# Final norm written whole, the last slot's tokens normed by themselves and written behind it; slot 31 run wholly behind slot 30

## The chip, the cores and the metric

One NeuronCore of a Trainium2 chip runs the whole kernel. The metric is the device time of one execution in microseconds; the time before is the median of three runs. "PE" is TensorE, "DVE" VectorE, "ACT" ScalarE, "POOL" GpSimd and "SP" SyncE; PEld is TensorE's weight load. A "q" behind an engine's name is its sequencer, which issues DMAs and waits on semaphores.

## What is computed

Two transformer blocks on 1024 tokens of width 1024, in float32. The change touches the end of the second one: the routed experts' sum is added to the residual, and every token is normed.

```python
def hierarchical_moe(h, ...):          # 32 experts, two per token
    ...
    out = lax.map(run_block, ...)       # (silu(x @ w_gate) * (x @ w_up)) @ w_down
    out = out * slot_gate[:, None]
    y = jnp.zeros((n_tok, dm)).at[slot_tok].add(out, mode='drop')
...
        x = x + gate_f * hierarchical_moe(h, ...)
    return rms_norm_2(x, final_g)       # x * rsqrt(mean(x*x) + 1e-6) * final_g
```

## The kernel before

**Slots.** The second block's 32 experts are run one behind the other as slots, ordered by how many tokens chose them. The last six slots (26 to 31) hold at most 64 tokens each ("small", `HALF_AT`), two others at most 32. For a slot the kernel gathers its tokens' rows (POOL, `xg`), turns them (PE, line 541; ACT, line 543), multiplies them with the gate and up weights (line 556), applies Silu (line 671) and the product (line 672), turns the hidden rows, multiplies with the down weights, copies half of the result from PSUM (line 563), scales by the token's gate (lines 687, 688) and adds the rows into the residual `acc_d` in DRAM with an indirect accumulating DMA from POOL (line 518). Each such scatter waits until the one before it has landed.

**Weights.** Each weight matrix of a slot is loaded in two chunks of 1 MB; a small slot uses two gate, two up and two down chunks in fp32 as they are. `Loader` issues them on SP's queue in the order in which the units will run (`unit_order`, `queue_experts`), at most four in flight: load n waits until load n-4 has landed. Buffers come from four rings: two first ones (`rawA`, `rawS`, two buffers each) and two of five buffers behind them. `keep_first_rings(2)` keeps the last two chunks out of the first rings.

**Order of units.** `unit_order` puts slot i's down product behind slot i+1's gate and up products. So at the end it runs: gate/up of 30, down of 29, gate/up of 31, down of 30, down of 31. The order of every engine's instructions is the order in which the program emits them.

**The last slot.** When slot 30's scatter has been issued, `load_sums` (line 1409) takes the four buffers of the first rings as `xs`, eight residual tiles of 128 tokens, and issues their loads on SP (line 1407); these wait for slot 30's scatter to land. It also loads `final_g` on ACT's queue (line 1418) and builds `at`, a one-hot matrix from the last slot's tokens to their rows (lines 1424 to 1426). Slot 31's result isn't scattered: `keep_rows` (line 1430) splits it into a high and a low part, `rows`.

**The If.** Line 1449 is a branch on `nx`, the number of extra blocks needed when an expert has more tokens than its slots hold. Here it isn't taken. Every engine loads `nx` and branches, and behind it engines wait for some of their outstanding DMAs.

**The final norm.** Behind the If: for each tile, `add(tt)` adds `at` x `rows` to the residual tile. Even tiles are added on DVE from PSUM (line 1473), odd ones on PE with an identity matmul (lines 1466, 1468). ACT squares and sums (line 1476), Ln and Exp give the factor (lines 204, 205), DVE multiplies (line 1486), SP stores (line 1487). `add` runs two tiles ahead. `use_ln_exp` (line 155) loads ACT's function table ahead of it.

Of the kernel before, what the change touches and what calls it, by code (L numbers as in the profile page):

```python
# [21 lines left out]
P = 128  # L22
# [100 lines left out]
def kernel(ctx, tc, a, out):  # L123
# [38 lines left out]
    def bcast_row(ap, n):  # L162
        return bass.AP(tensor=ap.tensor, offset=ap.offset, ap=[[0, P], [1, n]])
# [421 lines left out]
    def run_experts(hlp, blocks, route):  # L585
# [1 line left out]

        n = len(blocks)
        units = []
        for i, kind in unit_order(n):  # L590
            units += [(i, kind, c) for c in blocks[i][kind]] if kind in "gud" else [(i, kind, None)]
        todo = deque((u[2][0], part) for u in units if u[2] is not None and not blocks[u[0]].get("small") for part in range(N_PARTS))
        hls, raws = deque(), {}
# [47 lines left out]
        def few(i, kind, c):  # L641

            nonlocal ps, gate_raw
            s = blocks[i]["subs"][0]
            m = s["m"]
            key, _, ci, n_ch, _ = c
            raw = ld.take(key)
            if key[2] == "g":
                gate_raw = key, raw
                if ci == 0:  # L650
                    ps = mm_ps()[:, 0]
                return
            if kind == "u":
                for b in range(4):
                    ex.product_few(s["xT"], (raw[:, b], gate_raw[1][:, b]), ps, ci * 4 + b, 7)
                ld.done(gate_raw[0])
            else:
                if ci == 0:
                    ps = mm_ps()[:, 0]
                for b in range(2):  # L660
                    ex.product_few(s["hT"], [raw[:, b, h * 512:(h + 1) * 512] for h in range(2)], ps, ci * 2 + b, 3)
            ld.done(key)
            for _ in range(N_PARTS):
                if len(hls) < N_SPLIT:
                    ahead()
            if ci < n_ch - 1:
                return
            if kind == "u":
                s["hid"] = hid = ex.tile("hid", [fd], ex.wide)[:m]
                if m == P // 2:  # L670
                    nc.scalar.activation(hid, ps[m:], AF.Silu)
                    nc.vector.tensor_tensor(hid, ps[:m], hid, op=OP.mult)
                else:
                    up = ex.few_sums(ps, m, (None, hid))
                    nc.scalar.activation(hid, hid, AF.Silu)
                    nc.vector.tensor_tensor(hid, up, hid, op=OP.mult)
                return
            if "keep" in s:
                upper = ex.tile("whole", [512], 1)[:m]
                ex.few_sums(ps, m, (None, upper))  # L680
                s["keep"](ps[:m], s, 0)
                s["keep"](upper, s, 1)
                return
            y = ex.tile("yo", [D], ex.wide)
            if m == P // 2:
                ex.few_sums(ps, m, (None, y[:m, 512:]))
                nc.vector.scalar_tensor_tensor(y[:m, :512], ps[:m], s["gate"][:m], ex.grow[:m, :512], op0=OP.mult, op1=OP.mult)
                nc.vector.scalar_tensor_tensor(y[:m, 512:], y[:m, 512:], s["gate"][:m], ex.grow[:m, 512:], op0=OP.mult, op1=OP.mult)
            else:
                ex.few_sums(ps, m, (y[:m, :512], y[:m, 512:]))  # L690
                nc.vector.scalar_tensor_tensor(y[:m], y[:m], s["gate"][:m], ex.grow[:m], op0=OP.mult, op1=OP.mult)
            ex.scatter(y, s["idx"], m)
            if "after" in s:
                s["after"]()
# [48 lines left out]
                    if "after" in s:  # L743
                        s["after"]()

    def unit_order(n):
        for i in range(n + 1):
            if i < n:
                yield from ((i, "g"), (i, "u"), (i + 1, "xT"))
            if i > 0:  # L750
                yield i - 1, "d"
            if i < n:
                yield i, "hT"
# [14 lines left out]
    dyn_ids, slot_row = {}, {}  # L768

    def queue_experts(blocks):  # L770
        for i, kind in unit_order(len(blocks)):
            for key, w, c, _, n in blocks[i][kind] if kind in "gud" else ():
                ld.queue(key, [P, 2048 // n, n], chunk_src(w, c, n))

# [371 lines left out]
    def block2(x_src):  # L1146
# [209 lines left out]
                b["u"] = [c for both in zip(b["g"], b["u"]) for c in both]  # L1356
                b["g"] = []
        queue_experts(blocks)
        keep_first_rings(2)
        s4 = ctx.enter_context(ExitStack())  # L1360

        def after_wo0():
# [8 lines left out]
        with ExitStack() as s3:  # L1371
# [37 lines left out]
            def load_sums():  # L1409
                ex, sub = lists[0][1], blocks[-1]["subs"][0]  # L1410
                m = sub["m"]
                assert not ld.todo and all(p[3] == 0 for p in ld.pools[:2])
                for pool in (rawA, rawS):
                    for _ in range(2):
                        xs.append(pool.tile([P, 2048], F32, tag="raw", name="raw").rearrange("p (t d) -> p t d", t=2))
                load_xs(nc.sync)
                fin["g"] = ex.tile("xg", [D], ex.n_x)
                nc.scalar.dma_start(fin["g"], bcast_row(a["final_g_2"], D))

                both = ex.tile("xT", [2, D], ex.wide, F32R)  # L1420
                rows, at = both[:2 * m, 0], both[:2 * m, 1]
                d = ex.tile("whole", [ex.fdim], 1)[:2 * m, :NT + 1]
                for i in range(2):
                    nc.vector.tensor_copy(d[i * m:(i + 1) * m, NT:], sub["idx"][:m])
                nc.vector.tensor_scalar(d[:, :NT], C["io"][:2 * m, 0:NT], -float(P), d[:, NT:], op0=OP.mult, op1=OP.add)
                nc.vector.tensor_tensor(at.rearrange("p (t c) -> p t c", t=NT), C["io"][:2 * m, None, :].to_broadcast([2 * m, NT, P]),
                                        d[:, :NT, None].to_broadcast([2 * m, NT, P]), op=OP.is_equal)
                fin["rows"], fin["at"], fin["y"] = rows, at, ex.tile("yo", [D], ex.wide)

            def keep_rows(ps, s, h):  # L1430
                m, rows = s["m"], fin["rows"]
                c = slice(h * 512, (h + 1) * 512)
                y = fin["y"][:m, c]
                nc.vector.scalar_tensor_tensor(y, ps[:m], s["gate"][:m], lists[0][1].grow[:m, c], op0=OP.mult, op1=OP.mult)
                nc.scalar.copy(rows[:m, c], y)
                nc.vector.tensor_tensor(rows[m:, c], y, rows[:m, c].bitcast(F32), op=OP.subtract)

            run_experts(hlp, blocks, route2)
            r, ex = lists[0]
            ld.drop_pools()  # L1440
            s4.close()

            nx = nc.values_load(r["nx"][0:1, 0:1], min_val=0, max_val=N_EXTRA)
            with ExitStack() as s5:
                ep = sub_pool(s5, "ep2")
                hlp = sub_pool(s5, "xhl3", bufs=3)
                ex3 = Experts(ep, ep, h_d[1], acc_d[1], None, 512, 1)
                ex3.grow = ex.grow
                with tc.If(nx > 0):
                    further = extra_lists(ep, r)  # L1450
                    with tc.For_i(0, nx, 1) as i:
                        extra_block(ex3, ep, hlp, i, further, *ws)
                    load_xs(nc.gpsimd)

            fp = sub_pool(s3, "fin")
            ss = fp.tile([P, NT], F32, name="ss")
            use_ln_exp()

            def add(tt):

                ps = mm_ps()
                x, s = xs[tt // 2][:, tt % 2], ss[:, tt:tt + 1]
                on_pe = tt % 2 == 1
                if on_pe:
                    for h in range(2):
                        nc.tensor.matmul(ps[:, h], ident, x[:, h * 512:(h + 1) * 512], start=True, stop=False)
                for h in range(2):
                    nc.tensor.matmul(ps[:, h], fin["at"][:, tt * P:(tt + 1) * P], fin["rows"][:, h * 512:(h + 1) * 512],
                                     start=not on_pe, stop=True)
                if on_pe:  # L1470
                    sums[tt] = flat(ps)
                else:
                    nc.vector.tensor_tensor(x, x, flat(ps), op=OP.add)
                    sums[tt] = x
                junk = fp.tile([P, D], F32, tag="junk", name="junk", bufs=2)
                nc.scalar.activation(junk, sums[tt], AF.Square, accum_out=s)
                rstd_of(s)

            sums = {}
            add(0)  # L1480
            add(1)
            for tt in range(NT):
                if tt + 2 < NT:
                    add(tt + 2)
                x, s = xs[tt // 2][:, tt % 2], ss[:, tt:tt + 1]
                nc.vector.scalar_tensor_tensor(x, sums[tt], s, fin["g"], op0=OP.mult, op1=OP.mult)
                nc.sync.dma_start(tok_tile(out[0], tt), x)

    gates_out = []

# [530 lines left out]
```

## Time and profile before

| | us |
|---|---|
| median of 3 runs | 2077.5 (2076.21 to 2079.62) |
| the profiled execution | 2075.67 |
| its span, first to last instruction | 2073.7 |
| slot 30's scatter issued | 2041.04 |
| residual loads issued from | 2046.51 |
| first / last product of the final norm starts | 2057.26 / 2067.88 |
| first / last output store issued | 2060.26 / 2069.19 |

All times of a trace count from the span's start. Over the whole span PE is busy 91%, PEld 72%, DVE 72%, ACT 50%, POOL 18%. A wait is put down by the profile to the last event that preceded its end, which need not be its cause.

### The profile page before, as it was taken

How to read it: one execution, taken by the hardware profiler on the slowest of the kernel's cores; microseconds unless marked ns; L12 is line 12 of the kernel's file. 1: busy time of each engine (PE TensorE's matmuls, PEld its weight loads, DVE VectorE, ACT ScalarE, POOL GpSimd, SP SyncE). 2: the span in 40 equal slices, each digit the busy share in tenths (PEclk: the TensorE clock that was granted, in tenths of full speed). 3: DMA queues.
4: the chain of work that ended last, by engine and by line, in shares of the span. 5: the costliest groups of instructions: out<-in, count | busy, mean ns of one | idle time of the engine just before them, and what ended most of it. 6: DMA issues, size and time to landing. Idle time of an engine off the chain costs nothing.

```text
span 2073.7 us, 25402 instructions
## 1 busy us (share of the span) xinstructions
PE 1895.3 (91%) x9192; PEld 1487.6 (72%) x9192; DVE 1500.4 (72%) x1934; ACT 1036.7 (50%) x1454; POOL 369.9 (18%) x300
## 2 busy tenths in 40 slices
PE   4999999949999999999969999899599999999885
PEld 3788888837888888888757787788488676776332
DVE  6699985466999999999844256676797768586214
ACT  4411123216788787878755244332386656465213
POOL 1045430032010101000010000000511314142210
PEclk7999999969999999999989999999799999999998
DMA  9467746288999999999532001335798999999997
GB/s 325 144 231 259 259 163 225 102 308 287 377 387 401 389 402 384 405 379 387 157 110 82 11 16 36 120 145 194 300 366 286 391 362 389 379 390 390 365 388 297
DMA packets 154108, 569.57 MB, mean 275 GB/s; under 512 B 31287, under 2 KB 54551, under 8 KB 104828
## 3 DMA queue, kind: packets, MB, share of 16 engines
q1 hardware_dynamic: 134812, 511.78, 64.3%
q0 software_dynamic: 18784, 55.46, 9.4%
q8 instruction: 73, 1.20, 0.2%
q10 hardware_dynamic: 384, 0.68, 0.1%
q14 instruction: 55, 0.45, 0.1%
HBM read 534.12 MB, written 42.66 MB: 278 GB/s over the span
## 4 chain that ended last, share of the span: by engine, by line
PE 76%; DMA 10%; DVE 9%; ACT 2%; issue 2%; POOL 0%; SPq 0%; DVEq 0%; ACTq 0%
PE mm L199 21%; PE mm L201 20%; PE mm L200 20%; DMA raw<-in_w_expert_up_dram 5%; DMA raw<-in_w_expert_down_dram 3%; DVE hl L192 2%; PE aux L533 2%; PE half L201 1%; PE half L200 1%; PE half L199 1%; PE aux L417 1%; PE mm L556 1%; PE aux L1599 1%; DVE adacc L301 1%; DMA raw<-in_w_expert_gate_dram 1%
## 5 line engine op out<-in xcount | busy, mean ns | idle before, releaser
L192 DVE TENSOR_TENSOR hl<-raw,hl 128x1024 fp32r<-128x1024 f32 x601 | 716.6, 1232 | 129.1 <-ACT hl L191 110.8
L191 ACT CAST hl<-raw 128x1024 fp32r<-128x1024 f32 x612 | 634.9, 1054 | 262.4 <-PE mm L201 228.2
L199 PE MATMUL mm<-hl,xT 128*128 128x512 f32 x832 | 327.8, 394 | 0.2 <-issue 0.2
L201 PE MATMUL mm<-hl,xT 128*128 128x512 f32 x832 | 325.2, 391 | 0.0
L200 PE MATMUL mm<-hl,xT 128*128 128x512 f32 x832 | 325.1, 391 | 0.0
L199 PE MATMUL mm<-hT,hl 128*128 128x512 f32 x448 | 178.7, 399 | 8.5 <-ACT hT L879 6.2
L201 PEld LDWEIGHTS mm<-hl,xT 128*128 128x128 f32 x832 | 156.6, 188 | 33.4 <-issue 0.4
L199 PEld LDWEIGHTS mm<-hl,xT 128*128 128x128 f32 x832 | 157.0, 189 | 32.5 <-issue 0.4
L200 PEld LDWEIGHTS mm<-hl,xT 128*128 128x128 f32 x832 | 156.7, 188 | 32.6 <-DVE hl L192 0.9
L200 PE MATMUL mm<-hT,hl 128*128 128x512 f32 x448 | 176.3, 393 | 0.5 <-DVE hT L880 0.5
L201 PE MATMUL mm<-hT,hl 128*128 128x512 f32 x448 | 176.0, 393 | 0.0
L199 PE MATMUL mm<-hl,hT 128*128 128x512 f32 x416 | 164.9, 396 | 0.2 <-ACT hT L195 0.2
L201 PE MATMUL mm<-hl,hT 128*128 128x512 f32 x416 | 162.6, 391 | 1.0 <-DVE hT L196 1.0
L200 PE MATMUL mm<-hl,hT 128*128 128x512 f32 x416 | 162.2, 390 | 0.0
L518 POOL DMA_INDIRECT acc_d<-yo,idx x35 | 64.3, 1836 | 259.1 <-DVE yo L741 118.2
L556 PE MATMUL mm<-raw,xT 128*32 128x512 f32 (+1 forms) x512 | 88.1, 630 | 21.6 <-DMA raw<-in_w_expert_up_dram 21.6
L199 PEld LDWEIGHTS mm<-hT,hl 128*128 128x128 f32 x448 | 85.1, 190 | 27.3 <-ACT hT L879 7.1
L301 DVE SCALAR_TENSOR_TENSOR adacc<-adaw,ccol,adacc 128x512 f32<-128x512 f32 x142 | 100.0, 770 | 0.0
L200 PEld LDWEIGHTS mm<-hT,hl 128*128 128x128 f32 x448 | 85.1, 190 | 18.9 <-DVE hT L880 1.5
L201 PEld LDWEIGHTS mm<-hT,hl 128*128 128x128 f32 x448 | 84.8, 189 | 17.9
L512 POOL DMA_INDIRECT xg<-h_d,idx x34 | 61.4, 1806 | 167.8 <-PE aux L541 112.6
L201 PEld LDWEIGHTS mm<-hl,hT 128*128 128x128 f32 x416 | 78.1, 188 | 17.9 <-DVE hT L196 1.4
(487 smaller groups left out, 3013.8 us busy)
## 6 DMA issues: line engine op xcount, KB each, us to landing
raw<-in_moe_w_gate_dram SPq DMA_DIRECT2D x64, 1024.0 KB
raw<-in_moe_w_up_dram SPq DMA_DIRECT2D x64, 1024.0 KB
raw<-in_moe_w_down_dram SPq DMA_DIRECT2D x64, 1024.0 KB
raw<-in_w_expert_gate_dram SPq DMA_DIRECT2D x64, 1024.0 KB
raw<-in_w_expert_down_dram SPq DMA_DIRECT2D x63, 1024.0 KB
raw<-in_w_expert_up_dram SPq DMA_DIRECT2D x62, 1024.0 KB
adaw<-in_ada_w_dram SPq DMA_DIRECT2D x47, 1024.0 KB
raw<-in_sc_w_in_dram SPq DMA_DIRECT2D x9, 1024.0 KB
```

What stands on the lines that cost most here:

```text
L191: nc.scalar.copy(hl[:, 0], raw)
L192: lo.tensor_tensor(hl[:, 1], raw, hl[:, 0].bitcast(F32), op=OP.subtract)
L199: nc.tensor.matmul(o, s_hi, m_hi, start=start, stop=False)
L200: nc.tensor.matmul(o, s_hi, m_lo, start=False, stop=False)
L201: nc.tensor.matmul(o, s_lo, m_hi, start=False, stop=stop)
L301: nc.vector.scalar_tensor_tensor(acc[kk % 2], w[:, k], c, add, op0=OP.mult, op1=OP.add)
L417: nc.tensor.matmul(o, xT[:, k], rsc[:, k], start=k == 0, stop=k == KC - 1)
L512: nc.gpsimd.indirect_dma_start(out=x[:m], out_offset=None, in_=self.src, in_offset=bass.IndirectOffsetOnAxis(ap=idx[:m], axis=0), bounds_c ...
L518: nc.gpsimd.indirect_dma_start(out=self.acc, out_offset=bass.IndirectOffsetOnAxis(ap=idx[:m], axis=0), in_=y[:m], in_offset=None, compute_ ...
L533: nc.tensor.transpose(ps[:, i * P:(i + 1) * P], self.block(x, k, tag), ident)
L556: nc.tensor.matmul(ps[at:at + m], sT[:, k], w, start=k < split, stop=k > last - split)
L1599: nc.tensor.matmul(ps[:, h * P:(h + 1) * P], a_, b_, start=True, stop=True)
```

## The change

Slot 30 is finished before slot 31 begins: `unit_order` gives its down product ahead of slot 31's gate and up products, and the six last chunks (four gate/up, two down of slot 31) are kept out of the first rings, since the residual is loaded into those as soon as slot 30 has been scattered. At that point POOL also gathers the residual rows of slot 31's tokens into `fin["x"]`.

The final norm then runs on the residual tiles without slot 31's contribution, in pairs of tiles (`normed`), ahead of the If, and all eight tiles are stored. Behind pair 1, slot 31's result is added to the gathered rows and these are normed too. When all eight stores have landed, POOL writes the normed rows over their places in the output with an indirect DMA. Should extra blocks be needed, the If's body scatters slot 31's result, runs them, and does the whole norm again.

```diff
-        for i, kind in unit_order(n):
+        for i, kind in unit_order(n, blocks[-1].get("small")):
...
             if "keep" in s:
                 upper = ex.tile("whole", [512], 1)[:m]
                 ex.few_sums(ps, m, (None, upper))
-                s["keep"](ps[:m], s, 0)
-                s["keep"](upper, s, 1)
+                s["keep"]((ps[:m], upper), s)
                 return
...
-    def unit_order(n):
+    def unit_order(n, alone=False):
+
         for i in range(n + 1):
+            if alone and i == n - 1:
+                yield i - 1, "d"
             if i < n:
                 yield from ((i, "g"), (i, "u"), (i + 1, "xT"))
-            if i > 0:
+            if i > 0 and not (alone and i == n - 1):
                 yield i - 1, "d"
...
-        for i, kind in unit_order(len(blocks)):
+        for i, kind in unit_order(len(blocks), blocks[-1].get("small")):
...
-        keep_first_rings(2)
+        keep_first_rings(6)
...
                 nc.scalar.dma_start(fin["g"], bcast_row(a["final_g_2"], D))
-
-                both = ex.tile("xT", [2, D], ex.wide, F32R)
...
+                fin["x"] = ex.tile("xg", [D], ex.n_x)[:m]
+                nc.gpsimd.indirect_dma_start(out=fin["x"], out_offset=None, in_=acc_d[1],
+                                             in_offset=bass.IndirectOffsetOnAxis(ap=sub["idx"][:m], axis=0),
+                                             bounds_check=T - 1, oob_is_err=False)
+
+            def keep_rows(parts, s):
+                m = s["m"]
+                fin["y"] = y = lists[0][1].tile("yo", [D], 2)[:m]
+                for h, p in enumerate(parts):
+                    c = slice(h * 512, (h + 1) * 512)
+                    nc.vector.scalar_tensor_tensor(y[:, c], p, s["gate"][:m], lists[0][1].grow[:m, c], op0=OP.mult, op1=OP.mult)
...
+            def normed(x, out_x, n):
+
+                p = x.shape[0]
+                ss = fp.tile([P, 2], F32, tag="ss", name="ss", bufs=4)[:p, :n]
+                for i in range(n):
+                    junk = fp.tile([P, D], F32, tag="junk", name="junk", bufs=2)[:p]
+                    nc.scalar.activation(junk, x[:, i], AF.Square, accum_out=ss[:, i:i + 1])
+                nc.scalar.activation(ss, ss, AF.Ln, bias=epsc[:p], scale=1.0 / D)
+                nc.scalar.activation(ss, ss, AF.Exp, scale=-0.5)
+                for i in range(n):
+                    nc.vector.scalar_tensor_tensor(x[:, i], x[:, i], ss[:, i:i + 1], fin["g"][:p], op0=OP.mult, op1=OP.mult)
+                    if out_x is not None:
+                        stores.append(nc.sync.dma_start(tok_tile(out[0], out_x + i), x[:, i]).ins)
...
+            stores = []
+            use_ln_exp()
+            for q in range(NT // 2):
+                normed(xs[q], 2 * q, 2)
+                if q == 1:
+                    nc.vector.tensor_tensor(fin["x"], fin["x"], fin["y"], op=OP.add)
+                    normed(fin["x"][:, None, :], None, 1)
+            rows = nc.gpsimd.indirect_dma_start(out=out[0], out_offset=bass.IndirectOffsetOnAxis(ap=last["idx"][:m], axis=0),
+                                                in_=fin["x"], in_offset=None, bounds_check=T - 1, oob_is_err=False).ins
+            behind(rows, stores)
+            stores.clear()
 
             nx = nc.values_load(r["nx"][0:1, 0:1], min_val=0, max_val=N_EXTRA)
...
                 with tc.If(nx > 0):
+                    ex.scatter(fin["y"], last["idx"], m)
                     further = extra_lists(ep, r)
...
                     load_xs(nc.gpsimd)
-
-            fp = sub_pool(s3, "fin")
...
+                    use_ln_exp()
+                    for q in range(NT // 2):
+                        normed(xs[q], 2 * q, 2)
+                    for st in stores:
+                        behind(st, [rows])
```

## Rows read from the trace of the kernel before

**Rows 1.** Busy time by stretch: PE, PEld, DVE, ACT, POOL, clock, DMA share, GB/s.

```profile
2010.00:2037.50 27.50, 21.58 (x104) 7.94 (x102) 2.77 (x4) 2.73 (x5) 2.59 (x2) 1.00 0.99 390
2037.50:2041.60 4.10, 3.58 (x19) 1.20 (x16) 2.16 (x6) 0.95 (x2) 0.56 (x1) 1.00 0.47 169
...
2048.00:2058.50 10.50, 8.24 (x18) 3.92 (x18) 4.03 (x5) 5.55 (x11) 0.00 (x0) 0.67 0.98 391
...
2061.00:2072.10 11.10, 4.15 (x12) 1.81 (x10) 8.16 (x7) 6.19 (x16) 0.00 (x0) 0.84 0.96 379
```

**Rows 2.** Scatters of slots 29 and 30: timeline, POOL's wait, chain of waits.

```profile
2025.01 1.40 POOL L518 DMA_INDIRECT acc_d<-yo,idx  x1 [13.82 <-DVE yo L688]
...
L518 POOLq EVENT_SEMAPHORE  x13: 17/17/17, 1872.5 to 2032.9; - x13
...
2041.04 5.46 DMA acc_d<-yo,idx
```

**Rows 3.** Timeline where the final norm starts: start, us, engine, line, operation, idle.

```profile
2050.34 1.22 DVE L1473 TENSOR_TENSOR raw<-raw,mm 128x1024 f32<-128x1024 f32 x1 [1.91 <-DMA raw<-acc_d]
...
2054.30 1.78 PE L1468 MATMUL mm<-xT 128*128 128x512 f32 x4
...
2056.12 1.22 DVE L1473 TENSOR_TENSOR raw<-raw,mm 128x1024 f32<-128x1024 f32 x1 [4.56 <-DMA raw<-acc_d]
```

**Rows 4.** Timeline: PE's waits for the second down chunks of slots 30 and 31.

```profile
2036.58 0.37 PEld L556 LDWEIGHTS mm<-raw,hT 128*64 128x64 f32 x4 [0.49 <-DMA raw<-in_w_expert_down_dram]
...
2041.58 0.20 PEld L556 LDWEIGHTS mm<-raw,hT 128*64 128x64 f32 x4 [0.69 <-DMA raw<-in_w_expert_down_dram]
```

**Rows 5.** Timeline: the load of `final_g` issued.

```profile
2038.81 0.36 ACTq L1418 DMA_DIRECT2D xg<-in_final_g_dram  x1
```

**Rows 6.** Timeline: a unit after a pause, then slot 31 from its last up chunk.

```profile
1975.17 5.35 PE L556 MATMUL mm<-raw,xT 128*64 128x512 f32 x16 [2.16 <-DMA raw<-in_w_expert_up_dram]
...
2031.61 3.65 PE L556 MATMUL mm<-raw,xT 128*64 128x512 f32 x16 [2.44 <-DMA raw<-in_w_expert_up_dram]
...
2035.31 0.59 ACT L671 ACTIVATE hid<-mm 64x512 f32<-64x512 f32 x1 [11.27 <-PE mm L556]
...
2035.94 0.68 DVE L672 TENSOR_TENSOR hid<-mm,hid 64x512 f32<-64x512 f32 x1 [11.21 <-ACT hid L671]
...
2038.63 0.69 PE L541 MATMUL aux<-ident,hid 64*128 64x64 f32 x4
...
2039.83 3.68 PE L556 MATMUL mm<-raw,hT 128*64 128x512 f32 x16 [0.52 <-ACT hT L543]
...
2043.56 0.58 ACT L563 COPY whole<-mm 64x512 f32<-64x512 f32 x1 [3.78 <-PE mm L556]
```

**Rows 7.** Timeline of ACT: a table load and what follows it.

```profile
1128.56 1.28 ACT L1242 ACT_TABLE_LOAD   x1
1129.85 2.01 ACT L1242 ACTIVATE y<-y 128x1024 f32<-128x1024 f32 x2
```

**Rows 8.** Timeline: one tile's factor on ACT; the last two products on DVE.

```profile
2057.38 1.06 ACT L1476 ACTIVATE junk<-raw 128x1024 f32<-128x1024 f32 x1
...
2058.56 0.29 ACT L204 ACTIVATE ss<-ss,epsc 128x1 f32<-128x1 f32 x1
...
2059.00 1.00 ACT L1476 ACTIVATE junk<-mm 128x1024 f32<-128x1024 f32 x1
...
2066.69 1.28 DVE L1486 SCALAR_TENSOR_TENSOR raw<-raw,ss,xg 128x1024 f32<-128x1024 f32 x1
2067.88 1.28 DVE L1486 SCALAR_TENSOR_TENSOR raw<-mm,ss,xg 128x1024 f32<-128x1024 f32 x1
```

**Rows 9.** The stores on SP's timeline; SP's drains at the program's end (ns, starts).

```profile
2060.26 9.26 SPq L1487 DMA_DIRECT2D out_dram<-raw  x8
...
L2017 SPq DRAIN  x3: 7/7/13, 2072.8 to 2073.1; - x3
```

**Rows 10.** POOL's semaphore update behind the If (ns; start).

```profile
L1449 POOLq INC_SWDGE_SEM  x1: 1626/1626/1626, 2046.8 to 2046.8; - x1
```

More of the change, by code (lines that the diff above doesn't have):

```diff
@@ L1418, in load_sums @@
                 nc.scalar.dma_start(fin["g"], bcast_row(a["final_g_2"], D))
-                both = ex.tile("xT", [2, D], ex.wide, F32R)
[L1421 to L1436, printed above, removed]
+                fin["x"] = ex.tile("xg", [D], ex.n_x)[:m]
[8 more added lines that the diff above has]
+                    nc.vector.scalar_tensor_tensor(y[:, c], p, s["gate"][:m], lists[0][1].grow[:m, c], op0=OP.mult, op1=OP.mult)
             run_experts(hlp, blocks, route2)
@@ L1441, in block2, with behind @@
             s4.close()
+            fp = sub_pool(s3, "fin")
+            last = blocks[-1]["subs"][0]
+            m = last["m"]
+            def normed(x, out_x, n):
[10 more added lines that the diff above has]
+                        stores.append(nc.sync.dma_start(tok_tile(out[0], out_x + i), x[:, i]).ins)
+            def behind(ins, earlier):
+                for e in earlier:
+                    tc.add_manual_dep(ins, e.name, DependencyInfo(DependencyClass.Sync, DependencyReason.DATA), reason="the same rows")
+            stores = []
[9 more added lines that the diff above has]
+            stores.clear()
             nx = nc.values_load(r["nx"][0:1, 0:1], min_val=0, max_val=N_EXTRA)
@@ L1453, in block2 @@
                     load_xs(nc.gpsimd)
-            fp = sub_pool(s3, "fin")
[L1456 to L1487, printed above, removed]
+                    use_ln_exp()
[3 more added lines that the diff above has]
+                        behind(st, [rows])
     gates_out = []
```

## Prediction

> **What bounds the kernel now.** I read the page first (span, engines), then the stretch table, then the timeline of the last 60 us, and last the waits of SP and POOL there. The page says PE 91% busy; that is an average over stages which the change leaves alone. What counts is the tail. [rows 1]: until 2037.5 us the DMA engines are full (0.99), so the slots' matmuls only follow the weights. Then their share falls (0.47 to 2041.6); they are full again with the residual's 4 MB from 2048 to 2058.5, and with the 4 MB of output from 2061 to 2072.1, and 1.6 us later the span ends. The reader should see two holes: 10.5 us ahead of the residual load and 2.5 us ahead of the stores. The first is made by slot 30's scatter [rows 2]: it is issued at 2041.04 and has landed 5.46 us later, at 2046.5, and only then does SP issue the residual's loads. The second is VectorE: `add(2)` on it stands ahead of the norm of tile 0 and starts at 2056.12 [rows 3]. That wait is put down to a DMA, but tile 1's and 2's matmuls run at the lower clock until 2056.1 (0.67 of full on average in 2048 to 2058.5), and the DVE add follows their end; from there VectorE is back to back until 2069.16.
>
> **The change, part by part.** Everything before slot 30's down product is untouched. I write u31b for the last gate/up chunk of slot 31, x for the residual tiles, fx for the last slot's own rows.
>
> *Weight order.* Now slot 31's four gate/up chunks come ahead of slot 30's two down chunks; afterwards behind them. Bytes and pace are the same (390 GB/s), so a chunk takes the landing time of whichever stood in its place. u31b moves from 2031.6 [rows 6] into the place where 30's second down chunk landed: 2036.6 [rows 4]. The last weight still lands near 2041.6. Keeping six chunks out of the first rings leaves them 10 buffers with 4 loads in flight; no load waits for a buffer. Price 0, and if that cover went, one chunk time, 2.6 us.
>
> *`final_g`.* Its 0.5 MB load is issued behind slot 30's copy on ScalarE, now at 2038.81, in the hole [rows 5]. It moves to about 2028.5, into the full stretch: 0.5 MB at 390 GB/s is 1.3 us which everything behind it is later. Bounds 0 and 1.3; I take 1.3 because that stretch has no free share. So u31b lands at 2037.9.
>
> *Slot 30 and the residual load.* Slot 30's second down chunk takes the second of the four places, two chunk times (1 MB at 390 GB/s is 2.7 us) before 2031.6, so 2026.3; half a unit of matmuls, the copy and two products later, about 4 us, its `yo` is done near 2030. POOL may not issue that scatter before slot 29's has landed, 2032.9 [rows 2]. It then takes 5.46 us (idle DMA) to 7.9 us (slot 29's, under load: 2025.01 to 2032.9): landed by 2038.5 to 2041. SP has by then issued all weights (the last one waits for the chunk four places before it, about 2033), so x starts at 2041 instead of 2046.5 and 4 MB take 10.4 us as now. The gather of fx waits for the same landing on POOL, where nothing is queued that anybody needs; it has until 2058.
>
> *Who gets the 5.5 us?* Nobody, at first: on ScalarE the norm stands behind all of slot 31, and that is later. Slot 31 loses its cover (slot 30's down product, which now hides its transposes). By [rows 6]: u31b to `Silu` 3.70, to hid 1.31, transposes and copy to the first down matmul 1.2, 16 matmuls 3.73, copy 0.58, small gaps 0.1: 10.6 us, 2048.5. Now the same copy ends at 2044.1. Then the table load, 1.28 us, which today lies beside the wait for x: ScalarE starts on x at 2049.8. By then pair 0 has landed (2041 + 1.5 + 2.6, even with the 4 us that the slowest DMA engine lags: 2049.1).
>
> An earlier table load starts at 1128.56 and takes 1.28 us, and the next activation starts at 1129.85 [rows 7]: nothing stands between them. The Trainium skill, "ScalarE: Activation LUTs", What ACT_TABLE_LOAD costs, gives a load of about the same size plus a drain of 1.38 us with each switch of set; by it the end would be 1.4 us later. The rows show none behind the load, and they decide.
>
> *The norm.* Removed: all matmuls of lines 1466 and 1468, four adds, the one-hot and the split rows; so the PE clock no longer matters there. The new order costs ScalarE per pair two squares of 1.18 us with their read, and Ln and Exp, 0.44 to the next start: 2.80 us, against 3.24 for two tiles now [rows 8]. VectorE needs two times 1.19, so ScalarE sets the pace. Pairs 0 and 1: 2049.8 to 2055.4. Then fx stands in both queues: its add waits on VectorE for both products of pair 1 (2.5 us with the handover) and takes 1.22 itself [rows 3], and ScalarE's square of fx waits for the add: idle from 2055.4 to 2059.2, then 1.62 of its own, 2060.9. Pairs 2 and 3 end at 2066.5, the last product at 2069.1. That is the time at which it ends now (2069.16).
>
> *The tail that is added.* The last store goes out at 2069.2 as now; its packets end at 2072.1 and the final drains run from 2072.8 [rows 9], so POOL, which waits for all eight stores, starts at about 2072.2. Queued behind that wait are POOL's load of `nx`, the branch, and the end of the program, for which all engines wait. The plain indirect write isn't in the trace. Bounds: 5.46 us for the accumulating one on a quiet DMA, 3.8 us from the first x load's issue at 2046.5 to its first use at 2050.34 [rows 3]; I take 4.6: 2076.8. Now the If stands in the hole ahead of the norm; behind its branch POOL waits for its DMAs and spends 1.63 us on a semaphore update, from 2046.8, 0.3 us behind the scatter's landing [rows 10]. At the end nothing covers this: 0.3 + 1.63, bounds 0 and 1.9, I take 1.9, the row of the same block: 2078.7. End barrier 0.9 as now: 2079.6.
>
> The Trainium skill, "DMA: Bandwidth & Descriptors", Anatomy of one DMA, fits such a transfer by 2.0 us plus bytes over 436 GB/s; an estimate for 64 rows of 4 KB by that page is 2.6 us, which would end the kernel 2 us earlier. The one quiet indirect write of this trace took 5.46, so I stay with the rows.
>
> **Sum.** 2037.9 + 10.6 + 1.3 (start on x) + 16.7 (four pairs, fx and its stall) + 2.6 (last product) + 3.1 (last store) + 4.6 + 1.9 + 0.9 = 2079.6 against 2073.7: 5.9 us longer. The profiled execution took 2075.67, so 2081.6 beside it; the median of the runs shown is 2077.5, so I forecast 2083.4.
>
> **Rivals.**
> 1. *The weight stream loses its lag; not slower.* Bytes run at full rate until 2037.5 but the last chunk is usable only at 2041.58 and the share is 0.47 in between [rows 1, 4]: one slow DMA engine is 4 us behind. If the new order lets it catch up, u31b lands 4 us earlier and all of the sum moves with it: 2079.4. It decides from a lag under 2.2 us on. Against it: slot 29's scatter and its small packets stay where they are, slot 30's comes on top.
> 2. *The tail is cheap.* The plain write lands in 3.8, and the If's update is run while it flies: 1.9 + 0.8 less, 2080.7. For it: nothing of POOL needs that order; against it: today's waits on POOL come ahead of the update.
> 3. *A cold PE.* With pauses of over 2 us ahead of it, a 16 matmul unit takes 5.35 instead of 3.65 at 1975 [rows 6]. After 2027.7 such pauses surround u31a, u31b and the down product. One or two units at half clock cost 1.7 to 3.4: 2085.1 to 2086.8.
> 4. *The overlap comes true.* If ScalarE could start on x as it lands, near 2045, and pair 2 stood ahead of fx, 3 to 5 us would go. Program order on ScalarE speaks against it: all of slot 31 is issued first. Even rivals 1 and 2 with a free `final_g` give together 2075.4, within 0.2% of now; being faster needs a term that I don't see.
>
> **How the numbers follow.** 0.2% is 4.2 us here, about what a measurement of this kernel can tell from no change, so slower begins at 2081.7. Forecast 0.58 (a sixth of it, with short tail terms, falls under 2081.7), rival 1 0.13, rival 2 0.11, rival 3 0.10, rival 4 or a gain unseen 0.08. Slower 0.48 + 0.10 = 0.58, same 0.10 + 0.13 + 0.11 = 0.34, faster 0.08. The range goes from 2077.0 (rival 1 with most of rival 2) to 2089.0 (rival 3 in full with the slow end of the scatter and the spread).
>
> **What the profile would show.** Slot 31's Silu at about 2041.6 (with u31b landed at 2037.9), x loads issued at 2041, the table load at 2048.5, ScalarE idle for 3.8 us ahead of the square of fx, the last product at 2069, POOL's indirect write at 2072, and after it 1.6 us of POOL's update. The forecast is wrong if u31b lands by 2034, if ScalarE squares x before slot 31's last copy, or if the span ends within 3 us of the write's issue.

## The result, and the profile after

The changed kernel takes 2092.93 us in the median (2087.42 to 2094.58) beside 2076.21 us of the kernel before: ratio 1.0072, 95% interval 1.0059 to 1.0085. Run again beside other variants it took 2090.25 us against 2076.16: ratio 1.0070 (1.0057 to 1.0083). It is about 15 us slower; 2083.4 was forecast, with a range to 2089.0.

The span of its profiled execution is 2091.1 us, 17.4 longer than before. First the lead: how late this execution already was ahead of everything altered. The load of slot 30's second up chunk is the same instruction in both. The kernel before, SP's timeline:

```profile
2004.42 0.33 SPq L92 DMA_DIRECT2D raw<-in_w_expert_up_dram  x1
```

The same load in the changed kernel:

```profile
2010.07 0.33 SPq L92 DMA_DIRECT2D raw<-in_w_expert_up_dram  x1
```

So 5.65 us of the 17.4 lie ahead of it, and 11.7 behind. From here on "lead" is that load's distance to 2004.42, and "behind" is a span less 2073.7 less its lead. The load is a good mark: less the lead, the products on slot 31's last up chunk start between 2037.8 and 2037.9 in all seven profiled executions with the new order. The experiments below show what the lead is.

The stretch behind, in the changed kernel; columns as in [rows 1]:

```profile
2010.00:2043.50 33.50, 25.05 (x120) 9.35 (x120) 5.57 (x8) 4.83 (x9) 4.23 (x3) 1.00 1.01 400
2043.50:2049.50 6.00, 4.34 (x20) 1.61 (x20) 0.68 (x1) 0.74 (x2) 0.99 (x1) 1.00 0.45 104
2049.50:2060.20 10.70, 3.65 (x16) 1.06 (x16) 3.44 (x4) 6.85 (x13) 0.00 (x0) 0.79 1.01 365
2060.20:2066.50 6.30, 0.00 (x0) 0.00 (x0) 4.36 (x5) 2.50 (x8) 0.00 (x0) 0.50 0.95 389
2066.50:2070.80 4.30, 0.00 (x0) 0.00 (x0) 2.94 (x3) 4.24 (x10) 0.00 (x0) 0.50 0.01 6
2070.80:2077.00 6.20, 0.00 (x0) 0.00 (x0) 2.99 (x3) 0.57 (x3) 0.00 (x0) 0.50 0.87 342
2077.00:2091.10 14.10, 0.00 (x0) 0.00 (x0) 0.00 (x0) 0.00 (x0) 0.95 (x1) 0.50 0.07 14
```

The last line is the one to look at: 14.1 us in which POOL works for 0.95, no other engine at all, and the DMA moves next to nothing. In [rows 1] and [rows 9] the span ended 1.6 us behind the last packets. The line of 2066.50 to 2070.80 is the pause made by the last slot's rows: the output stops there.

The changed kernel's timeline from slot 31's last up chunk on; it answers to [rows 6] and [rows 8]:

```profile
2043.51 3.65 PE L556 MATMUL mm<-raw,xT 128*64 128x512 f32 x16 [3.22 <-DMA raw<-in_w_expert_up_dram]
...
2049.78 3.65 PE L556 MATMUL mm<-raw,hT 128*64 128x512 f32 x16 [0.52 <-ACT hT L543]
...
2053.48 0.58 ACT L563 COPY whole<-mm 64x512 f32<-64x512 f32 x1 [3.75 <-PE mm L556]
2054.08 1.28 ACT L155 ACT_TABLE_LOAD   x1
...
2055.38 1.06 ACT L1448 ACTIVATE junk<-raw 128x1024 f32<-128x1024 f32 x1
...
2063.20 1.21 DVE L1465 TENSOR_TENSOR xg<-xg,yo 64x1024 f32<-64x1024 f32 x1
2064.45 1.06 ACT L1448 ACTIVATE junk<-xg 64x1024 f32<-64x1024 f32 x1 [3.67 <-DVE xg L1465]
...
2071.47 2.48 DVE L1452 SCALAR_TENSOR_TENSOR raw<-raw,ss,xg 128x1024 f32<-128x1024 f32 x2 [0.16 <-ACT ss L1450]
...
2078.77 0.95 POOL L1467 DMA_INDIRECT out_dram<-xg,idx  x1 [29.27 <-SPq L1478]
```

Less the lead, the up chunk lands at 2037.9, ScalarE starts on the residual at 2049.7, the last product ends at 2068.3. Up to there the new way has lost nothing: before, VectorE ended at 2069.16. What is lost comes behind. POOL's instructions that aren't counted as busy, in the changed kernel, by line (durations in ns as minimum, median and maximum, then the first and the last start in us):

```profile
L1467 POOLq EVENT_SEMAPHORE  x5: 17/43/43, 2077.6 to 2078.0; - x5
...
L1478 POOLq EVENT_SEMAPHORE  x4: 17/43/43, 2079.3 to 2082.1; - x4
...
L1478 POOLq INC_SWDGE_SEM  x1: 1671/1671/1671, 2082.2 to 2082.2; - x1
...
L2018 POOLq DRAIN  x3: 52/103/6112, 2083.9 to 2090.5; - x3
...
L2018 ACTq DRAIN  x2: 8/8/8, 2072.6 to 2090.2; - x2
L2018 DVEq DRAIN  x2: 10/14/17, 2075.7 to 2090.3; - x2
```

POOL's wait for the stores ends at 2077.64, its write starts at 2078.77, and its wait for the write to land (line 1478) ends at 2081.98. Then it does the If's semaphore update of 1.67 us, as in [rows 10], and a drain of 6.11 us; nothing else runs. ACT's and DVE's own drains at the program's end take under 0.02 us. POOL's drain was there before too. The kernel before, same view:

```profile
L2017 POOLq DRAIN  x3: 52/103/5949, 2048.5 to 2073.4; - x3
```

There it took 5.95 us from 2048.5 on, beside the residual load, and cost nothing.

### The profile page after: what moved, and what is told of

Same layout as the page of the kernel before. It is cut to its first block, busy times and chain, and to the rows that moved or that the text cites. A ratio compares the mean times of both kernels' runs of the same rounds, so it can differ in the third digit from the quotient of the medians.

```text
span 2091.1 us, 25317 instructions
## 1 busy us (share of the span) xinstructions
PE 1884.7 (90%) x9160; PEld 1482.7 (71%) x9160; DVE 1495.9 (72%) x1926; ACT 1034.9 (49%) x1448; POOL 373.5 (18%) x302
```

## The experiments

The table has each run's median and ratio (against the kernel before, run on the same chip), and from its profiled execution the lead and what lies behind.

| run | median us | ratio | 95% interval | lead | behind |
|---|---|---|---|---|---|
| changed kernel | 2092.93 | 1.0072 | 1.0059 to 1.0085 | 5.65 | 11.7 |
| changed kernel again | 2090.25 | 1.0070 | 1.0057 to 1.0083 | 1.43 | 13.7 |
| e1, no write | 2078.10 | 1.0013 | 1.0002 to 1.0024 | 3.13 | 0.9 |
| e2, no If | 2085.51 | 1.0050 | 1.0033 to 1.0068 | -0.33 | 8.6 |
| e3, order alone | 2080.81 | 1.0021 | 1.0012 to 1.0030 | 1.37 | 3.1 |
| e4, norm alone | 2090.90 | 1.0070 | 1.0053 to 1.0086 | 2.28 | 13.4 |
| e5, rows last | 2083.61 | 1.0037 | 1.0023 to 1.0051 | 0.20 | 9.3 |
| e9, POOL stores last | 2079.62 | 1.0018 | 1.0009 to 1.0027 | 0.26 | 2.6 |
| e12, warm slot 31 | 2089.50 | 1.0060 | 1.0047 to 1.0074 | 3.52 | 11.9 |

**e1: no write.** The changed kernel without the rows' write.

```diff
-            rows = nc.gpsimd.indirect_dma_start(out=out[0], ...)
-            behind(rows, stores)
```

> Left out: the last slot's rows are not written over the output (nor ordered behind the stores); all else as changed. Tail theory: behind the last store POOL's write (4.0 us in flight), the If's semaphore update (1.7) and POOL's drain (6.1) stand one behind the other; without the write POOL does the last two early, beside the norm, and the program ends some 2 us after the stores have landed: 11 to 12 us shorter than the changed kernel, near 2081.4, the drain starting before 2070. Rival, the drain belongs to the program's end whatever POOL did before: only the flight goes, 4 to 5 us, near 2088.5. Rival, the loss lies ahead of the tail: under 4 us.

Measured: 2078.1 us; 0.9 us are left behind the lead. The drain starts early, in e1 by line:

```profile
L2013 POOLq DRAIN  x3: 52/103/6031, 2055.4 to 2077.5; - x3
```

The longest of the three is the first: it starts at 2055.4 and is over at 2061.5, 15 us ahead of the others. So the reordering and the whole new norm together cost what the interval says, 0.02 to 0.24%. All the rest of the loss is the write at the end and what it drags behind it. The tail theory holds; the rival that a drain of 6 us belongs to the end whatever POOL did is out.

**e2: no If.** The changed kernel with the write but without the load of `nx` and the If.

```diff
-            nx = nc.values_load(r["nx"][0:1, 0:1], min_val=0, max_val=N_EXTRA)
-            with ExitStack() as s5:
-                ...
```

> Left out: the If with the extra blocks and the load of nx (not taken with these inputs); the write of the last rows stays at the end. Theory A, POOL's 6.1 us drain is the wake of the If's semaphore update: drain under 1 us, about 8 us shorter than the changed kernel (1.7 + 6.1 + 0.5), near 2085. Theory B, the drain belongs to an indirect DMA shortly before the end: it stays near 6 us and only the update and the load go, 2 to 2.5 us, near 2090.5.

Measured: 2085.5 us. As a time that is theory A's 2085, which counted from the first median; from the changed kernel's second median it is 4.7 less, by the ratios 4.2, and the time alone doesn't decide. The drain does: it stays, so theory A (wake of the update) falls. e2, POOL's timeline, then its drains by line:

```profile
2074.08 0.95 POOL L1467 DMA_INDIRECT out_dram<-xg,idx  x1 [31.00 <-issue]
```

```profile
L2001 POOLq DRAIN  x3: 52/103/7287, 2073.9 to 2081.7; - x3
```

The long drain starts in the queue at 2073.86, just before the write does, and ends at 2081.15, 6.1 us behind the write's end. With the If the drain counts from the end of the update, and the update waits for the write to land. So the If adds the flight (2.3 us beyond POOL's own work) as well as the update's 1.7; theory B had only the update and the load. From the end of POOL's write to the span's end it is 11.4 us in the changed kernel and 7.0 here.

**The changed kernel again.** No edit.

> The changed kernel once more, unaltered. In its first profiled execution 5.4 us of the 17.4 us of longer span stood ahead of every altered instruction, read at SP's weight loads (1.2 us at 87, 3.4 at 510, 5.4 at 1922); the same loads stand at +2.2, -0.3, +1.6 and -0.6 us in the four variants of it run since, whose code up to there is the same. Theory, this part is chance: here between -1 and +4, with the part behind it again 12 us (up to 15 where the PE falls to its lower clock in slot 31), and a median of 2086 to 2091. Rival, it belongs to the program: again 5 or more, a median over 2092.

Measured: a median of 2090.25 us, in its profile a lead of 1.43 and 13.7 behind. The leads of all runs in the table go from -0.33 to 5.65, in kernels whose instructions up to there are the same, and the same kernel had 5.65 and then 1.43. So the 5.65 doesn't belong to the program, and 4.2 us of the first span went with it; what makes the lead no run shows. Of the two us more behind, 1.7 come from PE. The down unit of slot 31 in this second execution:

```profile
2039.23 3.65 PE L556 MATMUL mm<-raw,xT 128*64 128x512 f32 x16 [1.72 <-DMA raw<-in_w_expert_up_dram]
...
2045.50 5.35 PE L556 MATMUL mm<-raw,hT 128*64 128x512 f32 x16 [0.52 <-ACT hT L543]
```

5.35 instead of 3.65: PE was cold, that is at its lower clock, for part of it (the granted clock is 0.68 on average from 2045.50 to 2050.80, and 1.00 in the same unit of the first execution). The forecast's third rival came in beside its first line, in this execution and not in the first one. The idle time just ahead of the unit doesn't decide it: it is 0.52 us in both executions.

**e12: PE kept warm in slot 31.** Idle products ahead of its units.

```diff
+            if "keep" in s and key[2] != "g" and (ci == 0 or kind == "u"):
+                keep_warm(12 if kind == "u" else 3)
```

> The changed kernel with idle products (results unused) ahead of slot 31's two gate/up units and its down unit, to keep PE at the upper clock there. In its two profiled executions these units took 3.65 and 3.65 us (ahead of the last copy), then 3.65 and 5.35. Theory: no 5.35 left in slot 31's last two units, 1 to 3 us faster than the changed kernel in the median, near 2088.5. Rival, the idle products stand in the way of the real ones: 0 to 2 us slower.

Measured: both units take 3.65 us, 11.9 behind, and 2089.5 us in the median. That is 0.75 us under the changed kernel's second median, and the intervals of the ratios overlap: in the one profile the cold unit is gone, in the time it isn't resolved. The 1 to 3 us that were forecast aren't shown.

**e3: order alone.** The kernel before with the new `unit_order` and `keep_first_rings(6)`.

> The kernel before with the new order of units alone (slot 30 wholly ahead of slot 31, six chunks kept out of the first rings), the old norm by one-hot rows behind the If. My sum: the last slot's rows are ready 4 us later (2052.5), the residual is there 5.5 us earlier and no longer waited for; two adds with a cold PE take 5 us, VectorE's 13 us follow: the last product at 2070.5 instead of 2069.2, within -1 and +3 us of the kernel before. Rival, the earlier residual is worth all of its 5.5 us: 3 us or more faster. Rival, slot 31's lost cover is paid in full: 4 us or more slower.

Measured: 2080.8 us, 1.0021 (1.0012 to 1.0030), 4.4 us slower; my sum is missed and the rival (slot 31's lost cover paid in full) holds. The rows come later, and with them PE's part of the adds, in which PE is colder: its products for tiles 1 and 2 with the one-hot matrix take 2.58 us, and 1.78 before [rows 3]. e3, PE's timeline, then VectorE's:

```profile
2058.39 2.58 PE L1471 MATMUL mm<-xT 128*128 128x512 f32 x4
```

```profile
2053.38 0.69 DVE L1439 TENSOR_TENSOR xT<-yo,xT 64x512 fp32r<-64x512 f32 x1 [0.68 <-ACT xT L1438]
2056.00 1.22 DVE L1476 TENSOR_TENSOR raw<-raw,mm 128x1024 f32<-128x1024 f32 x1 [1.94 <-PE mm L1471]
2061.00 1.22 DVE L1476 TENSOR_TENSOR raw<-raw,mm 128x1024 f32<-128x1024 f32 x1 [3.78 <-PE mm L1471]
```

The second of these adds, the one from which VectorE is back to back, stood at 2056.12 before [rows 3]. It is 3.5 us later less the lead, though all of the residual had landed 4.3 us earlier (SP's last wait for it starts at 2056.7).

**e4: the norm alone.** The changed kernel with the old order (`unit_order(n)`, `keep_first_rings(2)`).

> The new norm and write with the old order of units (slot 31's gate and up ahead of slot 30's down; two chunks kept out of the first rings). My sum: slot 31 is done near 2044, but the residual lands 5 us later; ScalarE starts on pair 0 near 2050.7 instead of 2049.8 (both without what the profiled execution of the changed kernel had lost before the last slots), so within 1.5 us of the changed kernel: the new order brings nothing. Rival, the earlier residual load is worth its 5.5 us: 4 to 6 us slower than the changed kernel, near 2098. Rival, the order itself is what costs: 4 us or more faster, under 2089.

Measured: 2090.9 us, ratio 1.0070, as the changed kernel's. The residual comes later and ScalarE waits for it (its first square starts at 2051.45, 2.28 of it lead), but slot 31 is done earlier. The order brings nothing with this norm and costs 4 us with the old one (e3).

**e5: the rows last.** The changed kernel with the rows' norm behind pair 3.

```diff
                 normed(xs[q], 2 * q, 2)
-                if q == 1:
-                    nc.vector.tensor_tensor(fin["x"], fin["x"], fin["y"], op=OP.add)
-                    normed(fin["x"][:, None, :], None, 1)
+            nc.vector.tensor_tensor(fin["x"], fin["x"], fin["y"], op=OP.add)
+            normed(fin["x"][:, None, :], None, 1)
```

> The last slot's rows are normed behind pair 3 instead of behind pair 1. My sum: ScalarE no longer waits 3.7 us for the add nor spends 1.6 us on the rows ahead of pairs 2 and 3, the last store goes out 5.3 us earlier, the rows are ready 4.2 us behind the last product and 0.5 us behind the stores: 4.5 to 5 us shorter than the changed kernel, near 2088. Rival, the stores are bound by the DMA (two per 2.6 us) or the rows become the last thing: under 2 us.

Measured: 2083.6 us, ratio 1.0037: between 6 and 7 us better than the changed kernel's second median, more than summed, but within the intervals of the two ratios. In its trace the stores go out in 9.46 us, against 14.84 in the changed kernel (the two SP lines below, e5 and then the changed kernel), which is the 5.4 that ScalarE's pause and the rows' own 1.6 had cost.

```profile
2057.28 9.46 SPq L1454 DMA_DIRECT2D out_dram<-raw  x8
```

```profile
2059.47 14.84 SPq L1454 DMA_DIRECT2D out_dram<-raw  x8
```

Behind the lead this execution is 2.4 us better than the changed kernel's first one and 4.4 than its second. It had two cold units itself, slot 31's last up chunk (5.35) and its down unit (5.28), which hid 3.3 us of the gain from this view.

**e9 and e8: whose wake is the drain?** Two edits of the kernel before. e9 has POOL issue the last store; e8 gives POOL a copy of one column behind everything.

```diff
-                nc.sync.dma_start(tok_tile(out[0], tt), x)
+                (nc.gpsimd if tt == NT - 1 else nc.sync).dma_start(tok_tile(out[0], tt), x)
```

> The kernel before with the last of its eight stores issued by POOL instead of SP. It measures what a DMA of POOL's at the end costs by itself. In the four runs the drain ends 6.1 us after POOL's last software DMA instruction has ended. Theory: the store is issued near 2070 and the drain ends near 2076.3, 1.1 us of barrier behind it: 3 to 4.5 us slower than the kernel before. Rival, only an indirect DMA or the If's update has that wake: under 1.5 us.

Measured: 2079.6 us, 1.0018 (1.0009 to 1.0027), 3.5 us slower, as summed. e9, POOL's timeline, then its drains by line:

```profile
2069.05 0.63 POOL L1487 DMA_DIRECT2D out_dram<-raw  x1 [26.58 <-DVE raw L1486]
```

```profile
L2017 POOLq DRAIN  x3: 52/115/6691, 2069.0 to 2076.3; - x3
```

```diff
+            nc.gpsimd.tensor_copy(ss[:, 0:1], x[:, 0:1])
```

> The kernel before with one more POOL instruction behind everything, a copy of one column of the last normed tile: compute, no DMA. It asks whose wake the 6 us drain is. Theory, a software DMA's: POOL's last DMA is slot 30's scatter as before, its drain stays near 2048 and the end doesn't move (under 1 us). Rival, any work of POOL's: a drain of 6 us starts behind the copy at 2069.5 and the span is 2.5 to 3.5 us longer.

Measured: 2076.76 us, once, beside 2076.62, which says nothing by itself; the drain's place decides, and the theory of a DMA's wake falls. e8, POOL's timeline, then its drains:

```profile
2067.83 0.19 POOL L1488 COPY ss<-raw 128x1 f32<-128x1 f32 x1 [26.30 <-DVE raw L1486]
```

```profile
L2018 POOLq DRAIN  x3: 52/109/6184, 2067.8 to 2074.6; - x3
```

A copy of 0.19 us is enough: the drain starts in the queue at 2067.81 and ends at 2073.99, 6.0 us behind the copy's end. In e9 it ends 6.0 us behind the store's, in e2 6.1 behind the write's, in the changed kernel 6.1 behind the update's. So it isn't a DMA's wake: behind each of these four, the program's final drain of POOL ends 6.0 to 6.1 us later. Why it takes 6 us no run shows. The rival's size is missed: the span is 1.1 us longer than before and this execution's lead is -0.66, so 1.8 and not 2.5 to 3.5, in one execution.

**Towards a faster kernel.** e1 says that even a free write wouldn't make the changed kernel faster than the old one (e5's order wasn't run without its write, so that one stays open). So these start from the kernel before and go at its second hole. e6 adds tile 1 on VectorE, e13 has ScalarE issue the first three stores, e10 does that and keeps PE busy with idle products ahead of the adds.

```diff
-                on_pe = tt % 2 == 1
+                on_pe = tt % 2 == 1 and tt > 1
```

> The kernel before with tile 1 added on VectorE from PSUM, as the even tiles are, instead of by an identity product on the cold PE. The second hole of the profile before: VectorE waits until 2056.1 for PE. My sum: add(2) can go at about 2053.5, VectorE has 14.8 us of work from 2052 on, the last product starts near 2065.5 instead of 2067.9: 2 to 2.5 us faster. Rival, the stores and loads share the DMA engines and the end does not move: under 0.7 us.

Measured: 2075.89 us, 0.9999 (0.9990 to 1.0008). Two of VectorE's products come early, but then it waits 3.19 us, until 2059.6, for tile 4's product on PE. That stands behind tile 3, now the first one that PE adds, and PE is cold. And SP's first store goes out at 2060.05, since SP waits behind the If until the residual has landed (its last wait there is at 2059.9). e6, VectorE's timeline:

```profile
2053.94 2.48 DVE L1486 SCALAR_TENSOR_TENSOR raw<-raw,ss,xg 128x1024 f32<-128x1024 f32 x2
2059.60 1.22 DVE L1473 TENSOR_TENSOR raw<-raw,mm 128x1024 f32<-128x1024 f32 x1 [3.19 <-PE mm L1468]
```

```diff
-                nc.sync.dma_start(tok_tile(out[0], tt), x)
+                (nc.scalar if tt < 3 else nc.sync).dma_start(tok_tile(out[0], tt), x)
```

> The kernel before with the first three stores issued by ScalarE alone; PE cold as before. My sum: VectorE still starts at 2056.1 and ends at 2069.2, the last store goes out as before and only the backlog ahead of it is gone: 0 to 0.7 us faster. Rival, the late start of the stores on SP was the whole bound: 2 us faster.

Measured: 2076.65 us, 0.9999 (0.9990 to 1.0009). As summed, no gain: ScalarE's stores wait for VectorE ahead of its next squares, and four of the last five products each wait some 0.3 us for ScalarE.

```diff
+            keep_warm(16)
             add(0)
+            keep_warm(10)
             add(1)
```

> The kernel before with PE kept busy by idle products (results unused) up to the norm's adds, and the first three stores issued by ScalarE, whose queue isn't held at the If by the residual's loads. SP can't store before 2060 there, and the stores then fill the DMA for 10.6 us: that is the bound which e6 met. My sum: add(2) at 2053.5, three stores on their way by 2058.5, the last product starts near 2065.5 and the end is 2 to 2.5 us earlier than the kernel before. Rival, the 8 MB of loads and stores take the same DMA time and the end stays: under 0.7 us.

Measured: 2078.78 us, 1.0009 (1.0000 to 1.0018), if anything slower. The idle products stand behind the If with everything else, in the time in which the adds should run, and most of that time they are at the lower clock themselves. e10, PE's timeline, then the stretches from 2049.40 on with columns as in [rows 1]:

```profile
2049.44 5.30 PE L152 MATMUL mm<-onesB 128*128 128x512 bf16 x16 [4.34 <-ACTq L1449]
2054.39 0.82 PE L1468 MATMUL mm<-xT 128*128 128x512 f32 x2
```

```profile
2049.40:2050.50 1.10, 1.06 (x5) 0.48 (x5) 0.60 (x1) 1.05 (x1) 0.00 (x0) 1.00 1.04 425
2050.50:2053.90 3.40, 3.40 (x9) 1.20 (x8) 0.00 (x0) 0.23 (x1) 0.00 (x0) 0.50 1.02 417
2053.90:2054.40 0.50, 0.50 (x5) 0.24 (x3) 0.00 (x0) 0.00 (x0) 0.00 (x0) 0.97 1.01 418
```

Half of the sixteen run at the granted clock of 0.50. The first real product starts only at 2054.39, against 2047.88 before, and the first add on VectorE at 2055.25 instead of 2050.34 [rows 3]; the lead is 1.35 of that. The real products behind them do run at the upper clock (1.00 from 2054.40 to 2059.80), too late to help.

No version here beats the kernel before.

## Why the prediction was wrong, point by point

- **Direction, and most terms, right.** Less the lead: u31b at 2037.9 (forecast 2037.9; that the 1.3 us are `final_g`'s fits, but slot 30's scatter moved into the full stretch as well, and no run parts the two), 10.6 us to the slot's last copy (10.6), the residual's load issued at 2042.1 (2041; slot 29's scatter landed only at 2034.4 and not at 2032.9, which was still early enough), ScalarE on the residual at 2049.7 (2049.8), its pause ahead of the rows 3.67 (3.8), the last product's end 2068.3 (2069.1; a pair takes 2.65 us and not 2.80). Stores landed, by the wake of POOL's wait at 2077.64, 3.7 us behind the last issue (3.1); the write 4.3 (4.6), of which 1.1 pass before POOL's instruction starts and 3.2 from its start to the landing; the update with its semaphores 1.84 (1.9).
- **The step that failed is the last one: "End barrier 0.9 as now".** It is 7.25 us: 6.11 of POOL's drain and 1.1 of barrier. I read the end of the kernel before from SP's drain [rows 9], at a place where POOL's long drain had been over for 18 us. POOL's row, shown above for the kernel before (2048.5 on), stands in the same view as SP's. I had written that all engines wait for POOL there, and moved POOL's last work from 2046.8 to the end, but priced of that only what [rows 10] shows, one instruction of it. A drain that costs nothing while something covers it is a term as soon as the cover goes.
- **Rival 3 was no alternative but an addition.** The down unit was cold in one of the changed kernel's two executions, and slot 31's units in e2 and e5 too; that is 1.7 us per unit on top of the sum. Forecast 5.9, end barrier 6.35 more than taken, 0.5 saved in the other terms: 11.7, as in the first execution; with a cold unit 13.4, against 13.7 in the second. The rival's condition was too simple: it names pauses of over 2 us, but in [rows 6] the unit at 2031.61 takes 3.65 behind a pause of 2.44 us.
- **Rivals 1, 2 and 4** did not come: u31b landed in its forecast place, POOL's waits stand ahead of its update, and ScalarE squared nothing before slot 31's last copy. Rival 1's reason, one slow DMA engine, isn't in its rows: of the 0.7 MB that move from 2037.5 to 2041.6 (169 GB/s), 0.5 are `final_g`, issued in that stretch [rows 5].
- **The lead** was in no term. Executions differ by some us ahead of all that was changed, so one profiled execution of either kernel is no measure of a difference of 5 us. The first median, 2092.93, is the very execution that was profiled, with a lead of 5.65; the leads of the other four aren't known. With the drain priced the forecast would have been 2083.4 + 6.35 = 2089.8. That this is within 0.5 of the second median is partly luck, since cold units (1.7 us each, in the executions that have them) aren't in the sum.
- **The Trainium skill's two rules.** The first square on the residual starts 0.02 us behind the end of the table load at 2055.36. By the Trainium skill, "ScalarE: Activation LUTs" (What ACT_TABLE_LOAD costs), it would start 1.4 us later; the trace doesn't agree. The write takes 3.2 us from the start of POOL's instruction at 2078.77 to the end of the wait for it at 2081.98. The estimate from the Trainium skill, "DMA: Bandwidth & Descriptors" (Anatomy of one DMA), was 2.6 us; it is 0.6 short, and 1.7 short of the 4.3 from the wake of POOL's wait on.

## What to carry to other kernels

Before moving an engine's last work to the end of a kernel, look at what that engine does behind it now, in the rows that aren't counted as busy: the drain, the semaphore updates, the waits. Here 0.2 MB written by POOL behind all else cost 4.3 us from wake to landing, 1.8 of update and 6.1 of drain, while the same drain was free before. An overlap is only worth what the next engine in program order can use of it: the residual's load was issued 4.4 us earlier (2047.71 less the lead, against 2046.51), and the queue that needed it stood behind the slot that it was meant to overlap.

## What the runs showed of the hardware

- POOL's final drain ends 6.0 to 6.1 us behind the last thing that POOL executed, be it a copy of 0.19 us (e8), a direct store of 0.63 (e9), an indirect write of 0.95 (e2) or the semaphore update of 1.67 (the changed kernel).
- Executions of the same instructions reach the same load between 0.66 us earlier (e8) and 5.65 us later (the changed kernel) than the profiled execution of the kernel before did.
- Sixteen idle products meant to warm PE, behind 4.34 us without work, took 5.30 us in e10; the granted clock was 1.00 in their first 1.1 us, 0.50 in the next 3.4 and 0.97 behind that.
- A plain indirect write of 0.2 MB by POOL on a quiet DMA landed 3.2 us behind the start of its instruction (the changed kernel).
